# A hybrid encoder block on one core: retention rotates without the row factor, and the setup is laid out anew

## The chip, the cores and the metric

The kernel runs on one core of one Trainium2 chip. A core has a matrix engine (TensorE, PE in the profile; its weight loads are PEld), a vector engine (VectorE, DVE), an activation engine (ScalarE, ACT), a general engine (GpSimd, POOL) and an engine that here only starts transfers (SyncE, SP). Each engine takes its instructions in a fixed order. The metric is the device time of one execution, in microseconds (us).

## The reference

Sixteen learned meta tokens are put ahead of 1024 positions of width 1024 (T = 1040 rows). One layer follows: a root-mean-square norm, one combined input projection, a branch A of bidirectional retention in four heads (chunks of 128 rows), a branch B of windowed attention in eight heads, two gates, an output projection, a second norm and a residual add. Cut to what the change touches:

```python
u = _rms_norm(h, pre_w)          # row i of x*pre_w times r_i = rsqrt(mean(x_i^2) + eps)
z = u @ w_in                     # rq, rk, rv, rg, aq, ak, av, ag, gr, ga
rq = _rotary(rq, pos); rk = _rotary(rk, pos) * RET_DK ** -0.5
# retention, forward: out_i = sum_{j <= i} (q_i . k_j) * gamma^(i-j) * v_j, and backward likewise
o_r = (o_r - mean) * rsqrt(var + EPS)   # per row and head
```

The factor r_i of a row is one number, so it can be applied to the result of a projection instead of to its input.

## The kernel before

All matrix products are made from fp32 values split in a rounded high part and a remainder: `mm3` (L68) issues three matmuls, high by high (L70), low by high (L71) and high by low (L72). x stands in memory transposed, in eight blocks of 128 channels by 1040 rows. The kernel is written as one sequence of operations, and a planner at compile time gives each engine its fixed order from that sequence and its own estimate of times.

**Setup (L213 to L311).** SyncE starts all loads: the norm weights `vec`, the decay parameters `dect`, the weight of the first retention head in four parts (`w0_part`), x block by block (`xr`, six buffers), the constants `tabt` (identity, two distance tables and five index columns `idx`), and the rotation tables `cr` and `sr`. For each block k ScalarE writes the high part `xh` (L268), VectorE the low part `xl` (L269), and TensorE adds the block's share to the six outputs of head 0's keys (four pieces) and queries (two halves) (`qk0_mm`, 18 matmuls a block). Those six outputs take six of the eight accumulator banks: two of the three in the group `pj`, one of two in `p1`, both in `p2`, the one in `p3`. ScalarE also squares each block (L274), and the squares are added up in two sums, `sq[0]` on VectorE and `sq[1]` for the last three blocks, there on GpSimd (L278). 36 matmuls with a single column of ones (18 calls, L285) turn the sums into the mean square of each row, `ms`; GpSimd raises it to the power -0.5 (`rcol`, L288). The last block's `qk0_mm` stands behind that in the text.

GpSimd computes the retention decays from `dect` (`decays`, L173): two powers, a series in about twenty tiny operations on 128x8 tiles, six scaled exponents `ex`, and (`decay_columns`, L198) one power that gives the table of columns `dtab`. `decay_table` (L203) makes the 128x128 decay mask `DT` of a head from `lg`, on VectorE and ScalarE.

`rcol` is a column. For each chunk it is spread over a tile by ScalarE (`rw`) and turned by a matmul with the identity (L303) into a row over all partitions, `rbc`, which VectorE multiplies into `cr` and `sr` (L305, L306). The rotation of a projected piece (`rope_evac`, L151) then applies the row factor along with the angle: three VectorE instructions into `m1` and `m2` (two buffers each) and an add on GpSimd (L158).

**Retention (L364).** For each head: `stage1` projects a value chunk (`projT`, 24 matmuls into a `pj` bank; for chunk 0, the 16 meta rows, 16 matmuls, gathered by a ScalarE copy and a VectorE add, L138 and L139), scales it with `rcol` and splits it (`vh`, L394; `vl`, L395), turns the key chunk, forms the scores and splits them and the decayed keys. `stage2` makes the inner product, the product with the forward state and the new state. A backward sweep follows, with the per-row norm. Between the steps of the sweep `fill()` puts pieces of the next head's projection (`gen_qk`). Weights come through `load_w` in two halves, rounded on GpSimd (L75) or on ScalarE, the remainder on VectorE (L78).

After retention come attention, then four projection phases; the change does not touch them.

Of the kernel before, what the change touches and what calls it, by code (L numbers as in the profile page):

```python
# [12 lines left out]
D = 1024  # L13
SEQ = 1024
NM = 16
# [12 lines left out]
SQ2 = 5  # L28
# [11 lines left out]
def block_kernel(ctx: ExitStack, tc: tile.TileContext, xT, x, w_in, w_rb, w_ab, w_out, vecs, dec, sink,  # L40
# [36 lines left out]
    def dve_lo(o, i, hi):  # L77
        nc.vector.tensor_tensor(o, i, hi.bitcast(F32), ALU.subtract)  # L78
# [72 lines left out]
    def rope_evac(t, a, b, o, nm):  # L151
# [5 lines left out]
        nc.vector.tensor_tensor(m2[0:64, 0:n], t[64:128, 0:n], sr[64:128, a:b], ALU.mult)  # L157
        nc.gpsimd.tensor_tensor(o[:, 0:n], m1[:, 0:n], m2[:, 0:n], ALU.add)  # L158

# [5 lines left out]
    warm, ones = (ra.tile([P, 1], F32, name=n) for n in ("warm", "ones"))  # L165
    dect, neg1, neg, na, e, e2, s_, ss, acc, lg = (ra.tile([P, 8], F32, name=n) for n in (
        "dect", "neg1", "neg", "na", "e", "e2", "s_", "ss", "acc", "lg"))
    ecst, ex = (ra.tile([P, 28], F32, name=n) for n in ("ecst", "ex"))
    ms = ra.tile([P, 9], F32, name="ms")
# [3 lines left out]
    def decays():  # L173
# [3 lines left out]
        nc.vector.memset(neg1, -1.0)  # L177
# [4 lines left out]
        g.tensor_scalar(e2, e, 2.0, 1.0, op0=ALU.add, op1=ALU.mult)  # L182
        g.tensor_tensor(e2, e2, neg1, ALU.pow)
# [28 lines left out]
    pv0 = {}  # L212
    with tc.tile_pool(name="setup", bufs=1, reuse_waits="tile") as st:  # L213
        nc.sync.dma_start(vec, vecs)
        nc.sync.dma_start(dect, dec.partition_broadcast(P))
        xr = [st.tile([P, T], F32, tag="xr", bufs=6, name=f"xr{k}") for k in range(KT)]
# [15 lines left out]

        w0_part(0, 1)
        nc.sync.dma_start(xr[0][:, 0:528], xT[0, :, 0:528])
# [5 lines left out]
        nc.sync.dma_start(tabt, tab[:, MW:])  # L240
        nc.sync.dma_start(xr[3], xT[3])
        w0_part(4, 8)
        nc.sync.dma_start(xr[4], xT[4])
        nc.sync.dma_start(xr[5], xT[5])
        nc.sync.dma_start(xr[6], xT[6])
        nc.sync.dma_start(xr[7], xT[7])
# [7 lines left out]
        sq = []  # L254
# [6 lines left out]
        nc.vector.memset(ones, 1.0)  # L261
        nc.vector.memset(ms, 1.0)
        decays()
        for k in range(KT):
            t = xr[k]
            parts = [(0, 528), (528, T)] if k == 0 else [(0, T)]
            for a, b in parts:
                nc.scalar.activation(xh[k][:, a:b], t[:, a:b], AF.Copy, scale=vec[:, k:k + 1])  # L268
                nc.vector.scalar_tensor_tensor(xl[k][:, a:b], t[:, a:b], vec[:, k:k + 1], xh[k][:, a:b].bitcast(F32),  # L269
                                               op0=ALU.mult, op1=ALU.subtract)  # L270
            if k < KT - 1:
                qk0_mm(k)
            q_ = st.tile([P, T], F32, tag="sq" if k else "sq0", bufs=4 if k else 1, name=f"sq{k}")
            nc.scalar.activation(q_, t, AF.Square)  # L274
            if k in (0, SQ2):
                sq.append(q_)
            else:
                (nc.gpsimd if k > SQ2 else nc.vector).tensor_tensor(sq[-1], sq[-1], q_, ALU.add)  # L278
        decay_columns()

        pms = p1("pms")
        for c in range(9):
            a, b = cols(c)
            for i in range(2):
                nc.tensor.matmul(pms[0:b - a, c:c + 1], sq[i][:, a:b], ones, start=i == 0, stop=i == 1)  # L285
    nc.vector.tensor_scalar(ms[0:NM, 0:1], pms[0:NM, 0:1], 1.0 / D, EPS, op0=ALU.mult, op1=ALU.add)
    nc.vector.tensor_scalar(ms[:, 1:9], pms[:, 1:9], 1.0 / D, EPS, op0=ALU.mult, op1=ALU.add)
# [4 lines left out]
    wv0 = load_w(w_in, U_V, act=True)  # L292
# [1029 lines left out]
```

## Time and profile before

| | us |
|---|---|
| median of 3 runs | 1105.4 (1105.38 to 1106.14) |
| the profiled execution | 1106.03 |
| its span | 1104.3 |
| TensorE busy | 1074.6 (97%) |
| VectorE busy | 869.5 (79%) |
| ScalarE busy | 487.4 (44%) |
| GpSimd busy | 257.5 (23%) |

The span is the stretch of the profiled execution from its first to its last instruction; the time of the execution lies 1.7 us around it. A row of a timeline gives start, duration, engine, line, operation, output and inputs with their shapes, and in brackets how long the engine had stood still and which engine's work ended that. `[2.66 <-DVE w L78]` is a wait of 2.66 us that ended when VectorE had written w at line 78. The granted clock is the share of full speed that TensorE's clock had in a stretch.

### The profile page before, as it was taken

What the parts mean: (1) busy time and instruction counts of PE and PEld (TensorE: products, weight loads), DVE (VectorE), ACT (ScalarE), POOL (GpSimd) and SP (SyncE); (2) the same over time, 40 slices, a digit from 0 to 9 for tenths busy, and PEclk for the clock granted to TensorE, in tenths of its full rate; (3) what the DMA queues carried; (4) which work ended last, traced back from release to release, by engine and by line L of the source; (5) the groups of instructions that cost most, each with busy time, mean ns of one, the idle gap of its engine ahead of it and who ended that gap; (6) DMA issues with size and microseconds to landing.
All of it is one profiled execution on the core that took longest, in us unless ns stands there. A gap on an engine that the chain in (4) does not pass through costs nothing.

```text
span 1104.3 us, 17280 instructions
## 1 busy us (share of the span) xinstructions
PE 1074.6 (97%) x5994; PEld 928.2 (84%) x5994; DVE 869.5 (79%) x1840; ACT 487.4 (44%) x1131; POOL 257.5 (23%) x378
## 2 busy tenths in 40 slices
PE   6899999999999999999999999999999999999996
PEld 5799999999988988988888788888888788787885
DVE  6487887878976798988667876888889889867765
ACT  7132241422513544544557644455457546433442
POOL 7532433324232244445220000000000000010032
PEclk9799999999999999999999999999999999999999
DMA  7201111101114971021114753779883765779463
GB/s 285 77 1 39 58 58 39 46 32 63 54 48 127 350 248 58 21 96 39 65 46 158 257 200 105 229 245 338 273 290 122 229 207 191 234 199 335 119 114 77
DMA packets 75656, 159.45 MB, mean 144 GB/s; under 512 B 7985, under 2 KB 19761, under 8 KB 74801
## 3 DMA queue, kind: packets, MB, share of 16 engines
q1 hardware_dynamic: 72112, 152.06, 40.1%
q0 software_dynamic: 3456, 6.29, 3.7%
q8 instruction: 47, 0.77, 0.3%
q14 instruction: 41, 0.33, 0.1%
HBM read 105.89 MB, written 52.43 MB: 143 GB/s over the span
## 4 chain that ended last, share of the span: by engine, by line
PE 87%; DVE 4%; DMA 3%; POOL 2%; ACT 1%; issue 1%; SPq 1%; POOLq 0%; DVEq 0%; ACTq 0%
PE bz L71 7%; PE bz L72 7%; PE bz L70 7%; PE paq L71 3%; PE paq L72 3%; PE paq L70 3%; PE bo L71 2%; PE br L71 2%; PE bo L70 2%; PE bo L72 2%; PE br L72 2%; PE br L70 2%; PE pv L70 2%; PE pv L71 2%; PE pv L72 2%; PE ba L71 2%
## 5 line engine op out<-in xcount | busy, mean ns | idle before, releaser
L961 POOL DMA_DIRECT2D mx_d<-c1a x4 | 3.7, 924 | 397.6 <-DVE c1a L952 394.3
L71 PE MATMUL bz<-big,llz 128*128 128x512 f32 x208 | 82.5, 397 | 0.4 <-DVE llz L78 0.3
L72 PE MATMUL bz<-big,lhz 128*128 128x512 f32 x208 | 81.9, 394 | 0.0
L70 PE MATMUL bz<-big,lhz 128*128 128x512 f32 x208 | 81.1, 395 | 0.0
L72 PE MATMUL pv<-wl,big 128*128 128x256 f32 x256 | 73.2, 286 | 0.0
L70 PE MATMUL pv<-wh,big 128*128 128x256 f32 x256 | 73.2, 286 | 0.0
L71 PE MATMUL pv<-wh,big 128*128 128x256 f32 x256 | 72.9, 285 | 0.0
L70 PE MATMUL bz<-T,lhz 128*128 128x512 f32 x156 | 61.8, 396 | 1.7 <-ACT T L659 1.3
L71 PE MATMUL bz<-T,llz 128*128 128x512 f32 x156 | 61.5, 394 | 0.0
L72 PE MATMUL bz<-T,lhz 128*128 128x512 f32 x156 | 61.3, 394 | 0.0
L78 DVE TENSOR_TENSOR wl<-wr,wh 128x1024 fp32r<-128x1024 f32 x34 | 47.6, 1401 | 14.0 <-POOL wh L75 14.0
L1112 ACT ACTIVATE p<-p,nm 128x400 f32<-128x400 f32 (+1 forms) x64 | 38.4, 600 | 38.8 <-DVE nm L1110 35.0
L1123 POOL TENSOR_SCALAR p<-p,den 128x400 f32<-128x400 f32 (+1 forms) x60 | 36.3, 615 | 71.9 <-DVE den L1118 49.1
L71 PE MATMUL paq<-big,wl 128*128 128x512 f32 x128 | 51.3, 401 | 0.0
L70 PE MATMUL paq<-big,wh 128*128 128x512 f32 x128 | 51.0, 398 | 0.0
L72 PE MATMUL paq<-big,wh 128*128 128x512 f32 x128 | 50.9, 397 | 0.0
L70 PEld LDWEIGHTS pv<-wh,big 128*128 128x128 f32 x256 | 48.9, 191 | 0.9 <-DVE vl L395 0.6
L72 PEld LDWEIGHTS pv<-wl,big 128*128 128x128 f32 x256 | 48.8, 190 | 0.1
L71 PEld LDWEIGHTS pv<-wh,big 128*128 128x128 f32 x256 | 48.8, 191 | 0.0
L71 PEld LDWEIGHTS bz<-big,llz 128*128 128x128 f32 x208 | 39.1, 188 | 9.8 <-DVE llz L78 0.9
L70 PEld LDWEIGHTS bz<-big,lhz 128*128 128x128 f32 x208 | 39.1, 188 | 9.4 <-ACT lhz L682 0.2
L72 PEld LDWEIGHTS bz<-big,lhz 128*128 128x128 f32 x208 | 39.2, 188 | 8.9
(609 smaller groups left out, 3670.8 us busy)
## 6 DMA issues: line engine op xcount, KB each, us to landing
wr<-in_w_in_dram SPq DMA_DIRECT2D x35, 512.0 KB, 3.6
wrz<-in_w_in_dram SPq DMA_DIRECT2D x28, 512.0 KB, 5.5
tg<-tg_d SPq DMA_DIRECT2D x32, 256.0 KB, 4.4
T<-preT SPq DMA_DIRECT2D x6, 1024.0 KB, 8.6
oTr_d<-ost SPq DMA_DIRECT2D x16, 256.0 KB, 2.2
xs<-in_xT_dram SPq DMA_DIRECT2D x16, 256.0 KB, 5.0
xsT<-xs SPq DMA_DIRECT2D x16, 256.0 KB, 4.8
oTa_d<-oa SPq DMA_DIRECT2D x16, 256.0 KB, 2.2
```

The source lines that it names most:

```text
L70: nc.tensor.matmul(o, ah, bh, start=first, stop=False, **kw)
L71: nc.tensor.matmul(o, al, bh, start=False, stop=False, **kw)
L72: nc.tensor.matmul(o, ah, bl, start=False, stop=last, **kw)
L78: nc.vector.tensor_tensor(o, i, hi.bitcast(F32), ALU.subtract)
L961: nc.gpsimd.dma_start(d, to, accum_op=ALU.add)
L1112: nc.scalar.activation(p[:, 0:wid], p[:, 0:wid], AF.Exp, scale=-1.0, bias=nm_[:, e_:e_ + 1], accum_out=den[:, e_:e_ + 1])
L1123: nc.gpsimd.tensor_scalar(pt[e_][:, 0:wid], pt[e_][:, 0:wid], den[:, e_:e_ + 1], 1.0, op0=ALU.mult, op1=ALU.mult)
```

## The change

The row factor leaves the rotation of retention. Queries and keys are rotated without it; the values carry its square (`r2`, the reciprocal of the mean square, on VectorE), and the output rows carry it once: in the copy of the inner product (`scale=rcol`) and in the query decay columns (`qd`, which now hold rcol times the decay, a column for each chunk). Score (i, j) lacks r_i and r_j, value j has r_j squared, row i gets r_i back.

Around that: all squares are added up on VectorE, in one sum that is then split in high and low parts, and 18 rounded matmuls with two columns of ones replace the 36. `decay_columns` comes right behind `decays`, and the second power in `decays` becomes a reciprocal on VectorE. The first half of x's first block, `dect` and the five index columns are loaded from ScalarE's queue; the tables of `tabt` come last; x has eight buffers. Head 0's first piece is rotated ahead of the split of the sum, the other five behind it, and on VectorE everything of retention comes behind the last of these (`issue_after(ins)` keeps what is written in its block behind `ins` on the engine of `ins`). The decay mask of head h + 1 is made at chunk 4 of head h. The row `rbc` is laid out in the second head, at chunks 2, 4 and 6, now by transposes, and multiplied into `cr` and `sr` ahead of the last head, since the later users of the rotation (attention) still need it.

```diff
         g.tensor_tensor(e, ecst[:, 0:8], na, ALU.pow)
-        g.tensor_scalar(e2, e, 2.0, 1.0, op0=ALU.add, op1=ALU.mult)
-        g.tensor_tensor(e2, e2, neg1, ALU.pow)
+        nc.vector.tensor_scalar(e2, e, 2.0, None, op0=ALU.add)
+        nc.vector.reciprocal(e2, e2)
...
+    def evac_qk0(*pieces):
+        if 0 not in qk:
+            qk[0] = [], ra.tile([P, 4, 272], F32, tag="kp", bufs=2, name="kr0")
+        q, kt = qk[0]
+        for i in pieces:
+            m0, a, b, t = (outs[2:] + outs[:2])[i]
...
+            rot = rope_evac(t, a, b, o, f"qk0_{i}")
+        return rot
...
-        nc.sync.dma_start(vec, vecs)
-        nc.sync.dma_start(dect, dec.partition_broadcast(P))
-        xr = [st.tile([P, T], F32, tag="xr", bufs=6, name=f"xr{k}") for k in range(KT)]
+        xr = [st.tile([P, T], F32, tag="xr", bufs=KT, name=f"xr{k}") for k in range(KT)]
...
+        nc.scalar.dma_start(xr[0][:, 0:528], xT[0, :, 0:528])
+        nc.scalar.dma_start(dect, dec.partition_broadcast(P))
+        nc.scalar.dma_start(idx, tab[:, MW + 3 * P:])
+        nc.sync.dma_start(vec, vecs)
         w0_part(0, 1)
-        nc.sync.dma_start(xr[0][:, 0:528], xT[0, :, 0:528])
...
-        nc.sync.dma_start(tabt, tab[:, MW:])
...
         nc.sync.dma_start(sr, rope[1])
+        nc.sync.dma_start(tabt[:, 0:3 * P], tab[:, MW:MW + 3 * P])
...
         decays()
+        decay_columns()
         for k in range(KT):
...
-            if k < KT - 1:
-                qk0_mm(k)
-            q_ = st.tile([P, T], F32, tag="sq" if k else "sq0", bufs=4 if k else 1, name=f"sq{k}")
+            qk0_mm(k)
+            q_ = st.tile([P, T], F32, tag="sq", bufs=4, name=f"sq{k}")
             nc.scalar.activation(q_, t, AF.Square)
-            if k in (0, SQ2):
-                sq.append(q_)
-            else:
-                (nc.gpsimd if k > SQ2 else nc.vector).tensor_tensor(sq[-1], sq[-1], q_, ALU.add)
-        decay_columns()
-
+            if sq is not None:
+                nc.vector.tensor_tensor(q_, sq, q_, ALU.add)
+            sq = q_
+        pack_meta()
+        wv0 = load_w(w_in, U_V, act=True)
+        evac_qk0(0)
+        sqh, sql = (st.tile([P, T], R, name=n) for n in ("sqh", "sql"))
+        nc.scalar.copy(sqh, sq)
+        split = dve_lo(sql, sq, sqh)
         pms = p1("pms")
         for c in range(9):
             a, b = cols(c)
-            for i in range(2):
-                nc.tensor.matmul(pms[0:b - a, c:c + 1], sq[i][:, a:b], ones, start=i == 0, stop=i == 1)
+            for i, t in enumerate((sqh, sql)):
+                summed = nc.tensor.matmul(pms[0:b - a, 2 * c:2 * c + 2], t[:, a:b], ones, start=i == 0, stop=i == 1).ins
...
+    nc.vector.reciprocal(r2, ms)
     nc.gpsimd.tensor_tensor(rcol, ms, mhalf[:, 0:9], ALU.pow)
-    qk0_mm(KT - 1)
-    pack_meta()
...
-    vmeta = ra.tile([NM, 256], F32, name="vmeta0")
-    pv0[0] = projT(wv0, 0, "pv0_0", vmeta)
-    for g, cs in enumerate(((0, 1, 2), (3, 4, 5, 6), (7, 8))):
-        t = p1(f"rb{g}")
...
+    def row_factors(cs):
+        t = p1(f"rb{cs[0]}")
...
             nc.scalar.copy(rw[0:n], rcol[0:n, c:c + 1].to_broadcast([n, P]))
-            nc.tensor.matmul(t[:, a - base:b - base], rw[0:n], ident[0:n, 0:n], start=True, stop=True)
+            nc.tensor.transpose(t[:, a - base:b - base], rw[0:n], ident[0:n, 0:n])
         nc.scalar.copy(rbc[:, base:b], t[:, 0:b - base])
-        nc.vector.tensor_tensor(cr[:, base:b], cr[:, base:b], rbc[:, base:b], ALU.mult)
-        nc.vector.tensor_tensor(sr[:, base:b], sr[:, base:b], rbc[:, base:b], ALU.mult)
-    decay_table((0,))
+    def turn_factors():
+        for t in (cr, sr):
+            nc.vector.tensor_tensor(t, t, rbc, ALU.mult)
...
-            nc.scalar.activation(vh[0:n], pv[0:n, 0:256], AF.Copy, scale=rcol[0:n, c:c + 1])
+            state["v"] = nc.scalar.activation(vh[0:n], pv[0:n, 0:256], AF.Copy, scale=r2[0:n, c:c + 1]).ins
...
-                nc.scalar.copy(o, pa[:, 0:256])
-                nc.vector.scalar_tensor_tensor(o, pa[:, 256:512], qdf(h), o, op0=ALU.mult, op1=ALU.add)
+                nc.scalar.activation(o, pa[:, 0:256], AF.Copy, scale=rcol[:, c:c + 1])
+                nc.vector.scalar_tensor_tensor(o, pa[:, 256:512], qdf(h, c), o, op0=ALU.mult, op1=ALU.add)
...
-        if h == 0:
-            decay_table((1, 2, 3))
...
+            if c == 4 and h < NH - 1:
+                decay_table((h + 1,))
+            if h == 1 and c in (2, 4, 6):
+                with tc.issue_after(state["v"]):
+                    row_factors({2: (0, 1, 2), 4: (3, 4, 5), 6: (6, 7, 8)}[c])
             stage2(c)
...
-    evac_qk0()
+    with tc.issue_after(split):
+        evac_qk0(1, 2, 3)
+        decay_table((0,))
+        rotated = evac_qk0(4, 5)
     for h in range(NH):
...
-        retention(h, fill)
-        drain()
+        with tc.issue_after(rotated):
+            if h == 0:
+                for i, j in enumerate((8, 12)):
+                    for k in range(NH):
+                        nc.vector.tensor_scalar(qd[:, NH * i + k], rcol[:, 1:9], dtab[:, j + k:j + k + 1], None,
+                                                op0=ALU.mult)
+            if h == NH - 1:
+                turn_factors()
+            retention(h, fill)
+            drain()
```

More of the change, by code (lines that the diff above doesn't have):

```diff
@@ L27 @@
 N_GATE = 3
-SQ2 = 5
 U_QK, U_V, U_G = 0, 4, 8
@@ L164, in block_kernel @@
     mask = ra.tile([P, MW], F32, name="mask")
-    warm, ones = (ra.tile([P, 1], F32, name=n) for n in ("warm", "ones"))
-    dect, neg1, neg, na, e, e2, s_, ss, acc, lg = (ra.tile([P, 8], F32, name=n) for n in (
-        "dect", "neg1", "neg", "na", "e", "e2", "s_", "ss", "acc", "lg"))
+    warm = ra.tile([P, 1], F32, name="warm")
+    ones, onef = (ra.tile([P, 2], t, name=n) for n, t in (("ones", R), ("onef", F32)))
+    dect, neg, na, e, e2, s_, ss, acc, lg = (ra.tile([P, 8], F32, name=n) for n in (
+        "dect", "neg", "na", "e", "e2", "s_", "ss", "acc", "lg"))
     ecst, ex = (ra.tile([P, 28], F32, name=n) for n in ("ecst", "ex"))
-    ms = ra.tile([P, 9], F32, name="ms")
+    ms, r2 = (ra.tile([P, 9], F32, name=n) for n in ("ms", "r2"))
+    qd = ra.tile([P, 2 * NH, NB], F32, name="qd")
     nc.vector.memset(warm, 0.0)
@@ L259, in qk0_mm @@
                     k == 0, k == KT - 1)
-        nc.vector.memset(ones, 1.0)
+        nc.vector.memset(onef, 1.0)
+        nc.vector.tensor_copy(ones, onef)
         nc.vector.memset(ms, 1.0)
         decays()
+        decay_columns()
         for k in range(KT):
@@ L318, in kdb, with qdf, qdb @@
         return dtab[:, 4 + h:5 + h]
-    def qdf(h):
-        return dtab[:, 8 + h:9 + h]
-    def qdb(h):
-        return dtab[:, 12 + h:13 + h]
+    def qdf(h, c):
+        return qd[:, h, c - 1:c]
+    def qdb(h, c):
+        return qd[:, NH + h, c - 1:c]
     def cdf(h):
```

52 lines of the change are left out of this document (22 added, 30 removed).

## The prediction

> **What bounds the kernel now.** I read the page's busy line first, then the waits of TensorE, then a table of stretches up to 51.6 us, then the timelines of TensorE, GpSimd and VectorE inside those stretches.
>
> ```profile
> span 1104.3 us, 17280 instructions
> PE 1074.6 (97%) x5994; PEld 928.2 (84%) x5994; DVE 869.5 (79%) x1840; ACT 487.4 (44%) x1131; POOL 257.5 (23%) x378
> ```
>
> TensorE is busy for 97% of the span, so a change pays only if it takes away TensorE's idle time, slow clock or work. The waits say where the idle time is (columns: total us, times, longest):
>
> ```profile
> PE pq L70 <- ACT big L268: 7.0, 1, 7.0
> PE pms L285 <- POOL sq L278: 4.1, 1, 4.1
> PE pq L71 <- DVE w L78: 2.7, 1, 2.7
> ```
>
> All three lie in the setup, where the diff lies. The stretches (us, busy time and count of PE, PEld, DVE, ACT, POOL, granted clock, DMA) show what they cost:
>
> ```profile
> 6.90:21.10 14.20, 14.09 (x78) 12.51 (x78) 9.52 (x14) 13.59 (x14) 11.79 (x24) 1.00 1.03 406
> 21.10:23.70 2.60, 0.00 (x1) 0.01 (x1) 2.60 (x6) 1.16 (x2) 2.60 (x3) 1.00 0.53 213
> 23.70:35.50 11.80, 11.77 (x61) 10.20 (x61) 10.58 (x21) 5.10 (x8) 11.48 (x8) 0.86 0.30 98
> 35.50:39.60 4.10, 0.00 (x1) 0.01 (x1) 0.00 (x0) 0.00 (x0) 4.02 (x3) 0.77 0.28 109
> 39.60:46.60 7.00, 7.00 (x35) 6.99 (x35) 1.23 (x1) 0.00 (x0) 0.96 (x1) 0.50 0.21 75
> 46.60:51.60 5.00, 5.00 (x24) 4.13 (x24) 1.45 (x3) 0.69 (x3) 2.84 (x2) 0.52 0.00 0
> ```
>
> At 35.5 every engine but GpSimd stops while GpSimd adds squares. Then 35 one-column matmuls of the sums take 7.0 us at half clock, and the next 24 run at half clock too. Next, TensorE's timeline:
>
> ```profile
> 6.95 0.77 PE L70 MATMUL pq<-big,w 128*128 128x512 f32 x1 [6.95 <-ACT big L268]
> ...
> 11.43 0.39 PE L70 MATMUL pq<-big,w 128*128 128x512 f32 x1
> ...
> 19.93 0.63 PE L70 MATMUL pq<-big,w 128*128 128x512 f32 x2
> ...
> 23.70 0.92 PE L71 MATMUL pq<-big,w 128*128 128x512 f32 x2 [2.66 <-DVE w L78]
> ...
> 27.16 0.55 PE L70 MATMUL pq<-big,w 128*128 128x512 f32 x1
> ...
> 52.81 0.28 PE L71 MATMUL pv<-wh,big 128*128 128x256 f32 x1
> ...
> 55.41 0.28 PE L72 MATMUL pv<-wl,big 128*128 128x256 f32 x1
> ...
> 58.91 0.28 PE L70 MATMUL pv<-wh,big 128*128 128x256 f32 x1
> ```
>
> The first block of 18 matmuls takes 11.43 - 6.95 = 4.48 us (it begins cold), the next three (19.93 - 11.43) / 3 = 2.83 each. From 52.81 to 55.41 lie 22 steps: 0.118 us per 256-column matmul, so 24 of them, one value chunk, take 2.84. The fourth value chunk, c3, starts at 58.91. That is my milestone: I ask when the changed kernel starts c3, because from there on TensorE has the same work ahead of it in both.
>
> **The change part by part.**
>
> *Start.* The first half of x0 leaves on ScalarE's queue instead of fourth on SP's, and its landing no longer sets the start; the weight does:
>
> ```profile
> 5.91 0.40 POOL L75 TENSOR_SCALAR w<-wr 128x256 fp32r<-128x256 f32 x1
> ...
> 6.56 1.66 POOL L183 TENSOR_TENSOR e<-e,neg 128x8 f32<-128x8 f32 x1
> ```
>
> GpSimd has the first rounded weight at 6.31, behind the first power of the decays, which the change leaves in place; so TensorE starts at about 6.4, 0.55 earlier. The three DMAs issued on ScalarE, the two freed places in SP's queue, the eighth x buffer and the later load of the tables are costed at nothing: ScalarE's first work on data waits for x0 anyway, and x7 and the tables are read only after 20 us. If x0 lands late, the start is 6.95 again and 0.55 is lost.
>
> *The 2.7 us wait for the weight's low part.* VectorE was in order behind the decay table of all heads:
>
> ```profile
> 20.83 0.51 DVE L206 TENSOR_SCALAR dd<-tabt,lg 128x128 f32<-128x128 f32 x2 [3.73 <-POOL lg L192]
> 21.25 1.26 DVE L278 TENSOR_TENSOR sq<-sq,sq 128x1040 f32<-128x1040 f32 x1
> 22.43 1.21 DVE L78 TENSOR_TENSOR w<-wr,w 128x1024 fp32r<-128x1024 f32 x1
> ```
>
> The table now comes behind the split of the squares, so this wait goes. What could be late next is VectorE itself. It gets seven adds of squares instead of four:
>
> ```profile
> L269 DVE SCALAR_TENSOR_TENSOR big<-xr,vec,big 128x1040 fp32r<-128x1040 f32 x7 | 9.2, 1324 | 0.7 <-ACT big L268 0.7
> L278 DVE TENSOR_TENSOR sq<-sq,sq 128x1040 f32<-128x1040 f32 x4 | 5.0, 1238 | 0.0
> L126 DVE CAST xm<-big 128x64 fp32r<-128x64 f32 x4 | 0.7, 183 | 0.0
> ```
>
> From about 9 us (an estimate: TensorE was at x1's block at 11.43, and x1 leaves two places earlier in SP's queue) it has 7 x 1.32 + 7 x 1.24 + 0.7 + 1.2 (two weight splits) = 19.8 us: done at 28.9, the last split of x at 27.7. TensorE's eight blocks, unstalled, end at 6.4 + 4.48 + 7 x 2.83 = 30.7. So VectorE stays ahead by 1 to 3 us; with less than that, TensorE would wait inside the blocks, and each us of it moves the milestone only if the handover below doesn't swallow it.
>
> *Sum of squares.* Gone are the two adds on GpSimd and their wait; new is a split (one instruction each on ScalarE and VectorE, on VectorE 1.24 like an add), and 18 rounded matmuls for 36. The old ones took 7.0 / 35 = 0.20 at half clock; I take 0.1 at full clock, 1.8 us, between nothing (hidden in idle time) and 18 x 0.2 = 3.6.
>
> *Handover.* Rotation no longer waits for the row factor, but VectorE does everything of retention only after the last of six rotations. Three banks are there for value chunks: c0 at once, c1 and c2 after the first and second rotation; c3 needs c0's bank, which VectorE frees (L139) behind the sixth. So c3 starts at R = end of rotations + the eight new query-decay columns + L139:
>
> ```profile
> 46.83 0.15 DVE L287 TENSOR_SCALAR ms<-pms 128x8 f32<-128x8 f32 x1
> ...
> 52.12 0.41 DVE L139 TENSOR_TENSOR vmeta<-pv,vmeta 16x256 f32<-16x256 f32 x1 [0.96 <-ACT vmeta L138]
> ...
> 54.33 0.43 DVE L155 TENSOR_TENSOR m_qk<-pk,cr 128x272 f32<-128x272 f32 x1
> ...
> 69.21 0.67 DVE L155 TENSOR_TENSOR m_qk<-pq,cr 128x512 f32<-128x512 f32 x1
> ```
>
> A rotation of a key piece is three such instructions, 1.3 us, of a query half 2.05. By VectorE alone: 28.9, four packing casts 0.7 and two value-weight splits 2.4 (32.0), first rotation 33.3, split 34.5, three rotations 3.9, sums and table 1.4 (an estimate: seven small instructions at about 0.2), two query rotations 4.1 (43.9), columns 1.2 and L139 0.4: R = 45.5.
>
> But each rotation ends in an add on GpSimd with two buffers, so the third rotation needs the first add, and GpSimd is busy with the decays:
>
> ```profile
> 10.39 1.18 POOL L185 TENSOR_TENSOR ss<-s__114 128x8 f32<-128x8 f32 x1
> ...
> 15.94 1.12 POOL L189 TENSOR_SCALAR acc<-acc 128x8 f32<-128x8 f32 x1
> ...
> 17.44 0.20 POOL L189 TENSOR_SCALAR acc<-acc 128x8 f32<-128x8 f32 x1
> ...
> 20.90 7.00 POOL L194 TENSOR_SCALAR ex<-lg,tabt 128x4 f32<-128x4 f32 x5
> 27.87 1.26 POOL L196 TENSOR_SCALAR ex<-lg 128x8 f32<-128x8 f32 x1
> 29.21 4.85 POOL L199 TENSOR_TENSOR dtab<-ecst,ex 128x28 f32<-128x28 f32 x1
> ...
> 55.75 0.77 POOL L158 TENSOR_TENSOR kr<-m_qk,m_qk 128x272 f32<-128x272 f32 x1 [5.85 <-DVE m_qk L157]
> ```
>
> A tiny operation takes 1.1 to 1.4 us while VectorE works and 0.20 while it stands still (it stood waiting from 17.1 to 20.8). In the changed kernel VectorE doesn't stand still. One power of 1.66 is gone, so ss comes at 8.7; it and 18 more operations at 1.12 end at 30.0. Of the six exponents three go at 1.4 (34.2); VectorE then soon waits for GpSimd, the rest run fast (35.2); the power 4.85 and two scales end at 40.5. First add 41.3; third rotation 42.6, fourth 43.9; the query rotations wait for the adds of these two, 46.0 and 48.1; plus 1.6: R = 49.5, taking rcol's power as fitting between.
>
> On this point the Trainium skill (GPSIMD Engine Reference, Specifications) says that GpSimd shares its SBUF interfaces with VectorE, with contention where VectorE reads two SBUF inputs. By that rule moving the squares to VectorE slows the decays put first on GpSimd, and the time is that of R = 49.5; if it didn't hold here, R = 45.5. The 1.12 against 0.20 above agrees with it.
>
> TensorE meanwhile has c0 (16 matmuls, 1.9), c1, c2 (2.84 each) and the sums (1.8): done at 30.7 + 9.4 = 40.1. It then idles for 9.4 us and restarts cold. The price of that: 12 matmuls after the 2.7 us wait took 27.16 - 23.70 = 3.46 against 2/3 x 2.83 = 1.89, so 1.6.
>
> *Row factors.* Nine transposes in the second head cost 9 x 0.118 = 1.1 on TensorE; their copies run on ScalarE (44% busy). Between nothing and 2.5 (if each comes cold).
>
> *VectorE later.* The factors' turn into the rotation tables at the last head is two instructions of 1.24; the tables of the other heads move inside the heads. I cost them at nothing because VectorE has gaps (79%); if the cover is gone it is 2.5.
>
> Sum: c3 earlier by 58.9 - 49.5 = 9.4, less 1.6 cold, less 1.1 transposes: 6.7 us. The profiled execution took 1106.03 us around its span of 1104.3, and the median of the runs, 1105.4, is 0.6 below it: 1106.0 - 6.7 - 0.6 = 1098.7.
>
> **The rivals.**
> 1. GpSimd doesn't hold the rotations (the adds stand ahead of the exponents in its queue, or these run faster): R = 45.5, gain 10.7, 1094.7. For it: VectorE's order alone allows it. Against it: decays come first in the program. Were TensorE never to wait (c3 at 40.1), the gain would be 17.7, 1087.7.
> 2. Given back at the head boundaries: the 2.5 us of the factors' turn, in front of the last head, fall on the chain. The three waits above are the only ones over 1.3 us of TensorE, which speaks for slack there; gain 4.2, 1101.2.
> 3. Slower: GpSimd's decays get slower still. One exponent took up to 2.66 us by the tile's view:
>
> ```profile
> L194 POOL TENSOR_SCALAR ex<-lg,tabt x5: 360/1319/2655, 20.9 to 25.2; 128x4 f32<-128x4 f32 x5
> ```
>
> Six at that price end at 46, the power at 51.2, R = 60.2, and c3 is 1.3 later than now: with 1.6 and 1.1 that is 4.0 slower, 1109.4. It decides when the decays end after 47.2 (R = 56.2); slower than the measurement can miss, after 49.4.
>
> **How the numbers follow.** Likeliest, as summed, 0.42 (own range 1096.5 to 1100.5); rival 1 0.27, TensorE never waiting 0.04; rival 2 0.13; rival 3 0.14, of which 0.03 within 0.2%. 0.2%, 2.2 us, is about what a measurement of this kernel tells from no change. Of rival 2, 0.02 is within that too. Faster 0.84, same 0.05, slower 0.11. The range runs from 1089.0 (most of rival 1) to 1104.5 (rival 2 and a little of rival 3), leaving 0.05 below and 0.14 above.
>
> **What would show it.** Right: TensorE starts near 6.4 and has no wait on w; eight blocks end near 31; the sums take under 2.5 us; then one wait of 4 to 10 us, released by VectorE's L139 or a value split, with VectorE itself waiting on GpSimd's adds; from c3 on waits as before. Wrong: TensorE waiting inside the eight blocks (VectorE too late with the splits), no wait at the handover, or new waits of over 1 us at the second and fourth head.

## The result, and the profile after

The changed kernel takes 1098.7 us (median of four runs, 1097.02 to 1099.49) against 1105.8 for the kernel before beside it (1105.38 to 1107.58): a ratio of 0.9931, with an interval of 0.9914 to 0.9948. The profiled execution took 1098.83 us around its span. Its busy line:

```profile
span 1097.0 us, 17210 instructions
PE 1069.3 (97%) x5967; PEld 923.3 (84%) x5967; DVE 873.3 (80%) x1851; ACT 490.2 (45%) x1132; POOL 258.5 (24%) x374
```

Of the 7.3 us that the span lost, 5.3 are TensorE's busy time (1074.6 to 1069.3), 2.0 its idle time. The largest waits of TensorE in the setup and at the handover to retention (total us, times, longest):

```profile
PE pq L69 <- POOL w L74: 4.6, 1, 4.6
PE tr L408 <- DVE m_qk L156: 2.8, 1, 2.8
PE pkv L71 <- DVE vl L405: 1.4, 1, 1.4
...
PE pv L69 <- DVE vmeta L138: 1.2, 2, 1.0
```

The wait for squares on GpSimd (4.1 us before) and the wait for the weight's low part (2.7) are gone (0.2 us of the latter is left); the 4.6 us are the start. The same stretches as a table (us, busy time and count of PE, PEld, DVE, ACT, POOL, granted clock, DMA):

```profile
4.50:30.90 26.40, 26.05 (x146) 23.02 (x147) 23.71 (x33) 19.32 (x20) 23.09 (x24) 1.00 0.74 289
...
35.70:37.60 1.90, 1.90 (x20) 1.88 (x19) 0.08 (x1) 0.00 (x0) 1.90 (x1) 1.00 0.00 0
...
38.40:41.50 3.10, 0.29 (x4) 0.12 (x3) 1.40 (x4) 0.00 (x0) 3.10 (x4) 1.00 0.00 0
41.50:45.00 3.50, 3.50 (x18) 3.50 (x18) 3.35 (x8) 1.03 (x3) 1.74 (x3) 0.53 0.00 0
45.00:48.40 3.40, 1.08 (x5) 0.46 (x4) 3.28 (x8) 0.37 (x1) 2.74 (x2) 0.98 0.02 5
48.40:55.00 6.60, 6.27 (x35) 5.81 (x35) 6.60 (x19) 2.09 (x6) 4.82 (x4) 0.74 0.47 156
```

The eight blocks run with 0.35 us of idle time, the sums take 1.8 us at full clock (35.78 to 37.60). Then TensorE stands still for 2.8 us, works 3.5 us at half clock, stands still for 2.3 us more in three pieces (0.69 us for the row sums, 0.70 for a rotated query, 0.99 for the add of the first value chunk), and runs slow again behind c3. The clock column reads 1.00 for the first block too, although its 256-column matmuls come 0.21 us apart there (8.53 to 8.95) and not 0.118, so it leaves the slow start out. TensorE's timeline:

```profile
4.56 0.76 PE L69 MATMUL pq<-big,w 128*128 128x512 f32 x1 [4.56 <-POOL w L74]
...
37.49 0.25 PE L305 MATMUL pms<-ones,sql 128*128 128x2 f32 x1
...
41.49 0.27 PE L408 MATMUL tr<-ident,kr 128*16 128x128 f32 x1 [2.81 <-DVE m_qk L156]
...
48.45 0.53 PE L69 MATMUL pv<-wh,big 128*128 128x256 f32 x1 [0.99 <-DVE vmeta L138]
```

c3 starts at 48.45, 10.45 us earlier than before (58.91). What held it there is read on GpSimd and on VectorE:

```profile
13.42 1.12 POOL L190 TENSOR_SCALAR acc<-acc 128x8 f32<-128x8 f32 x1
...
28.14 1.05 POOL L193 TENSOR_TENSOR lg<-lg,acc 128x8 f32<-128x8 f32 x1
...
32.79 4.82 POOL L200 TENSOR_TENSOR dtab<-ecst,ex 128x28 f32<-128x28 f32 x1
...
38.24 1.05 POOL L74 TENSOR_SCALAR wh<-wr 128x1024 fp32r<-128x1024 f32 x1
39.25 0.75 POOL L157 TENSOR_TENSOR kr<-m_qk,m_qk 128x272 f32<-128x272 f32 x1
```

```profile
40.04 0.42 DVE L154 TENSOR_TENSOR m_qk<-pk,cr 128x256 f32<-128x256 f32 x1 [4.26 <-POOL kr L157]
...
47.99 0.41 DVE L138 TENSOR_TENSOR vmeta<-pv,vmeta 16x256 f32<-16x256 f32 x1
...
51.60 0.19 DVE L309 RECIPROCAL r<-ms 128x9 f32<-128x9 f32 x1
52.67 1.59 DVE L651 TENSOR_SCALAR qd<-rcol,dtab 128x8 f32<-128x8 f32 x8
```

Decays at 1.1 us an operation, the power of the columns, the rounding of half of the next head's weight (1.05 us, not in the forecast), then the first add (done at 40.0), for which VectorE's third rotation waited 4.26 us; the add of the first value chunk (L138) right behind the last rotation.

The lead of 10.45 us is not the gain of 7.1 (1105.8 to 1098.7). Followed by the first matmul of each piece of later work, it is 4.4 us at head 1's keys, 10.4 at head 2's, 11.1 at head 3's (220.01 to 208.93), and only 6.0 at attention's keys (287.44 to 281.47); from there it stays at 6 to 7. A first matmul also moves when the planner changes the order, so one such lead alone says little (the two kernels lose next to nothing between the first two of these, and the lead still goes from 4.4 to 10.4). The drop from 11.1 to 6.0 is different: the loss there can be seen. It lies at the start of the last head. The stretch from 250 to 290 us holds it in both kernels; first before, then after, with TensorE's waits there:

```profile
250.00:290.00 40.00, 39.52 (x319) 37.66 (x318) 34.69 (x92) 13.86 (x40) 15.50 (x24) 1.00 0.21 67
```

```profile
250.00:290.00 40.00, 37.66 (x285) 36.20 (x284) 32.83 (x98) 15.85 (x49) 12.84 (x23) 0.91 0.18 63
```

```profile
PE to L491 <- DVE rs L521: 1.0, 1, 1.0
PE pb L69 <- DVE rs L521: 0.7, 1, 0.7
PE tr L408 <- ACT ost L496: 0.6, 1, 0.6
```

Before, 0.5 us of this stretch is idle. After, 2.3 us are idle and 37.66 us of work run at a mean clock of 0.91, 3.4 us lost: 5.7 against 0.5.

### The profile page after: what moved, and what is told of

Read it like the earlier page. It is cut to its first block, busy times and chain, and to the rows that moved or that the text cites. A ratio compares the mean times of both kernels' runs of the same rounds, so it can differ in the third digit from the quotient of the medians.

```text
span 1097.0 us, 17210 instructions
## 1 busy us (share of the span) xinstructions
PE 1069.3 (97%) x5967; PEld 923.3 (84%) x5967; DVE 873.3 (80%) x1851; ACT 490.2 (45%) x1132; POOL 258.5 (24%) x374
## 4 chain that ended last, share of the span: by engine, by line
PE 83%; DVE 7%; POOL 3%; DMA 3%; ACT 2%; issue 2%; SPq 1%; POOLq 0%; DVEq 0%; ACTq 0%
PE bz L70 7%; PE bz L71 7%; PE bz L69 7%; PE br L70 2%; PE bo L70 2%; PE bo L69 2%; PE br L69 2%; PE bo L71 2%; PE br L71 2%; PE paq L70 2%; PE paq L71 2%; PE paq L69 2%; PE ba L70 2%; PE ba L71 2%; PE ba L69 2%; PE pv L69 2%
## 5 line engine op out<-in xcount | busy, mean ns | idle before, releaser
L69 PE MATMUL pv<-wh,big 128*128 128x256 f32 x256 | 75.1, 293 | 1.3 <-DVE vmeta L138 1.2
L70 PE MATMUL pv<-wh,big 128*128 128x256 f32 x256 | 74.2, 290 | 0.0
L69 PEld LDWEIGHTS pv<-wh,big 128*128 128x128 f32 x256 | 50.4, 197 | 2.4 <-DVE vmeta L138 1.6
L70 PEld LDWEIGHTS pv<-wh,big 128*128 128x128 f32 x256 | 50.4, 197 | 0.0
```

The source lines that it names most:

```text
L69: nc.tensor.matmul(o, ah, bh, start=first, stop=False, **kw)
L70: nc.tensor.matmul(o, al, bh, start=False, stop=False, **kw)
```

## The experiments

All times of a run are set against the kernel before on the same chip; the intervals are of the ratio. One table for all of them, explained by the sections below. "Lost" is TensorE's idle time plus its busy time times one minus the granted clock, added up over windows of 1 us in the profiled execution, at four places: the setup (0 to 60 us), the start of the last head (250 to 290), the end of retention (340 to 365), and the first projection phase (590 to 700). "Cover" below is work of another piece that TensorE can do while a step waits for another engine.

| run | ratio [interval] | span | c3 | lost 0-60 | 250-290 | 340-365 | 590-700 |
|---|---|---|---|---|---|---|---|
| before | 1 | 1104.3 | 58.9 | 21.3 | 0.5 | 2.1 | 2.1 |
| changed | 0.9931 [0.9914, 0.9948] | 1097.0 | 48.5 | 14.7 | 5.7 | 1.5 | 2.1 |
| a0 changed, again | 0.9941 [0.9928, 0.9954] | 1097.7 | 48.8 | 15.5 | 5.3 | 1.8 | 2.1 |
| e1 turn late | 0.9945 [0.9932, 0.9957] | 1098.1 | 48.2 | 16.7 | 5.6 | 1.5 | 2.1 |
| e8 turn forced late | 0.9988 [0.9976, 1.0000] | 1104.2 | 48.4 | 16.7 | 3.7 | 6.4 | 5.5 |
| e13 the same, cover held | 0.9929 [0.9912, 0.9946] | 1095.6 | 48.2 | 15.6 | 2.1 | 4.0 | 2.1 |
| e2 spare buffers | 0.9990 [0.9979, 1.0001] | 1104.8 | 49.8 | 16.5 | 5.3 | 5.0 | 4.8 |
| e9 and splits behind | 1.0004 [0.9994, 1.0015] | 1104.2 | 46.7 | 13.5 | 5.2 | 5.0 | 6.5 |
| e15 the same, cover held | 0.9938 [0.9922, 0.9954] | 1098.9 | 46.0 | 12.1 | 5.8 | 2.5 | 2.5 |
| e10 both | 0.9919 [0.9906, 0.9933] | 1095.4 | 46.2 | 12.3 | 2.1 | 5.0 | 2.8 |
| e12 both, cover held | 0.9901 [0.9883, 0.9919] | 1093.6 | 46.0 | 12.8 | 2.1 | 3.8 | 2.1 |
| e5 reciprocal early | 0.9968 [0.9959, 0.9978] | 1099.0 | 48.4 | 15.2 | 4.0 | 5.1 | 2.1 |
| e3 no adds of squares | one run, 1098.13 us | 1096.3 | 44.7 | 12.5 | 4.0 | 5.0 | 2.3 |
| e4 sum not split | 0.9955 [0.9940, 0.9970] | 1099.5 | 51.2 | 17.0 | 4.3 | 4.0 | 2.1 |

Span less the four losses is 1071.8 to 1074.0 us in all runs of the changed program but one (e15, 1076.0), so these four places explain the spans within about 1 us of each other. Each row is one profiled execution: the setup's order is the same in the changed kernel, a0, e1, e8 and e13, and it lost 14.7 to 16.7 us there, so differences of 1 to 2 us at one place can come from the execution and not from the edit.

### The changed kernel again

> The changed kernel once more, beside the next three on the same chip, so that they can be set against it directly. All theories: 1098.7 us, within 0.7.

1099.58 us (1098.31 to 1100.05), 0.9941: 0.2 us above the expected range. The intervals of the two ratios overlap, so a difference of 0.1% between two runs is not read as an effect below.

### The turn of the row factors, put late (e1, e8, e13)

```diff
-            if h == NH - 1:
-                turn_factors()
             retention(h, fill)
...
+            if c == 4 and h == NH - 1:
+                turn_factors()
```

> The two VectorE instructions that turn the row factors into the rotation tables stand at the fifth chunk of the last head and no longer ahead of its first. Theory A (they delay VectorE's first work for the last head, and TensorE's several short idle times around 262 to 268 us, 2.3 us, and the half clock after them, 268 to 274 us, some 2.9 us, follow from that): 4 to 5 us faster than the changed kernel, 1094.2 (1093.5 to 1095.0), and idle and half clock there gone. Rival B (the loss at the last head comes from the order of the rest, the turn only lies beside it): 1098.7, within 0.7, and the same idle time at the last head with the turn gone from it.

1099.78 us: no change from the second measurement. But the planner had put the two instructions back to where they were, as VectorE's timeline of this run shows (245.53 and 248.47 in the changed kernel), so it tells nothing of theory A:

```profile
246.70 1.43 DVE L332 TENSOR_TENSOR cr<-cr,rbc 128x1040 f32<-128x1040 f32 x1
...
249.64 1.22 DVE L332 TENSOR_TENSOR sr<-sr,rbc 128x1040 f32<-128x1040 f32 x1
```

So the place was forced, behind the scaled values of the sixth chunk:

```diff
+            if c == 4 and h == NH - 1:
+                with tc.issue_after(state["vl"]):
+                    turn_factors()
```

> The same edit as in the run of the turn put late, but now held on VectorE behind the scaled values of the sixth chunk of the last head, since there the planner had put the two instructions back ahead of that head. With it the order on TensorE at the last head is again that of the kernel before: ten more matmuls of value chunks between the last products of the backward sweep. Theory A (the turn, 2.65 us of VectorE, late for the sweep, makes the planner use up TensorE's cover early, and the 2.3 us idle and 3.4 us of slow clock at the last head are its price): that stretch costs under 1 us, and the time is 4 to 5 us less than the changed kernel's, 1094.6 (1093.5 to 1096.0). Rival B (the loss there has nothing to do with the turn, or is replaced by another at the turn's new place): 1098.9, within 0.8.

1105.17 us, slower than the changed kernel by 0.5%, which neither theory gives. At the last head it did what theory A says, in part: the loss fell from 5.3 to 3.7 (2.1 of idle time, 1.6 of slow clock). TensorE's order there shows how (name, chunk and number of matmuls; `pb` are the products of head 2's backward sweep, `pv` head 3's value chunks, which are the cover):

```
before   pb_3x3 to_5x1 pv_6x16 to_4x1 pb_2x3 to_3x1 tr_0x1 pb_1x3
changed  pb_3x3 to_5x1 pv_6x6 to_4x1 pb_2x3 pb_1x3 to_3x1 tr_0x1
forced   pb_3x3 pv_5x5 pv_6x2 to_5x1 pv_6x10 to_4x1 pv_6x4 pb_2x3 pv_6x8 to_3x1 tr_0x1 pb_1x3
```

In the changed kernel the turn sits in the middle of the sweep's start: its first two products stand at 242.75 and 250.94, 8.2 us apart (256.91 and 260.31 before, 3.4 apart), and 62 matmuls of cover go in between. At the sweep's end, where each step waits for the norm of a chunk, 6 are left for 16. Then, in the forced run, two later places lost 8.0 us more:

```profile
PE to L494 <- DVE op L526: 2.7, 2, 2.5
PE po L69 <- ACT pbh L1180: 2.0, 1, 2.0
```

```profile
340.00:365.00 25.00, 21.80 (x157) 20.95 (x156) 16.38 (x42) 13.40 (x31) 3.08 (x8) 0.86 0.68 230
590.00:700.00 110.00, 106.20 (x477) 85.63 (x476) 83.44 (x151) 60.33 (x120) 0.30 (x1) 0.98 0.52 177
```

The order shows these two as well. At the end of retention the last head's last product had no cover behind it (`pav` is attention's value projection), and the first projection (`bz`) began when attention's blocks `po_4` to `po_7` were still to do; in the changed kernel, `po_6` and `po_7`:

```
changed  pb_1x3 pavx5 to_3x1 pavx10 to_2x1 pavx7 to_1x1 ps_0x2
forced   to_3x1 pavx3 pb_1x3 to_2x1 to_1x1 ps_0x2
```

Nothing in the edit touches either place; the planner works out one order for the whole program and came to another. The next run holds the cover there, twelve matmuls of the third value chunk behind the last `pb`:

```diff
         for k in range(KT):
-            mm3(t[0:b - a, 0:256], ...
+            with tc.issue_after(last_pb[0]) if k >= hold else ExitStack():
+                mm3(t[0:b - a, 0:256], ...
```

> The run with the turn held late (1105.2), and now twelve matmuls of the attention's third value chunk are held on TensorE behind the last product of the last head's backward sweep; with them TensorE's order from there to the first projection phase is the changed kernel's again. Theory A (the turn's late place did help at the last head, and the 8 us that run lost came from two later places, 3.4 us idle with 2.7 us of slow clock around 346 to 356 us and the first projection begun before the attention's third last block): at the last head the lead of 1 us over the changed kernel is kept to the end, 1098.4 (1097.6 to 1099.2). Rival B (the loss has another cause, which the twelve matmuls don't touch): 1103 or more.

1098.89 us beside 1107.3 of before: 0.9929 [0.9912, 0.9946], in theory A's range. At the first projection the order is the changed kernel's again, and the 590 to 700 us loss is back at 2.1. At the end of retention it is not quite: the last `pb` has the twelve matmuls behind it, where the changed kernel has 22, and a wait of 1.3 us is left. At the last head the slow clock is gone, but not by this edit: TensorE's order and its waits there are those of the run before (two of 0.9 us and two of 0.2), which were followed by 1.6 us of slow clock in that execution and by none in this one.

```profile
250.00:290.00 40.00, 37.88 (x307) 36.31 (x306) 36.32 (x99) 17.70 (x56) 13.69 (x22) 1.00 0.15 54
340.00:365.00 25.00, 22.74 (x175) 22.02 (x174) 14.51 (x35) 14.51 (x33) 2.82 (x6) 0.93 0.77 265
```

```profile
PE to L497 <- DVE op L529: 1.3, 1, 1.3
```

From head 3's keys to attention's keys this run takes 69.6 us, the changed kernel's second run 72.2, and the loss from 250 to 290 us is 3.2 us less (1.6 in the run before). So the turn in its old place, with the order that came of it, costs 1.6 to 3.2 us. But 2.2 us are lost again at the end of retention (4.0 for 1.8), and the times of the two can't be told apart.

### No wait for GpSimd's first add (e2, e9, e15)

```diff
-        m1 = ra.tile([P, 512], F32, tag="m1", bufs=2, name=f"m1_{nm}")
-        m2 = ra.tile([P, 512], F32, tag="m2", bufs=2, name=f"m2_{nm}")
+        if spare:
+            m1, m2 = o, ra.tile([P, 512], F32, tag="q", bufs=6, name=f"m2_{nm}")
...
+            rot = rope_evac(t, a, b, o, f"qk0_{i}", i in (2, 3))
```

> The rotations of the third and fourth key piece of head 0 write their products into the output and into a spare buffer, so that they need not wait for GpSimd's first add (40.0 us, behind the decays). Theory A (this wait of 4.3 us on VectorE sets the end of the rotations and with it the start of the fourth value chunk c3): the two rotations run at 35.5 to 38.2, the query rotations from 40.0 to 44.2, c3 starts at about 44.6 for 48.45, and the time is 3.9 us less than the changed kernel's, 1094.8 (1094.0 to 1095.8). Rival B (something else holds the query rotations or c3, GpSimd's adds above all, or the lead is spent at a head's boundary): c3 at 46.5 or later, or c3 early and the time still 1097.5 to 1099.

1104.97 us, and c3 at 49.81, later than without the edit: neither theory's time, and rival B's late c3. The rotations did end at 44.2, as theory A says; then the planner put other work ahead of the row sums and L138, and TensorE waited 6.88 us behind it. VectorE's timeline (this kernel's L159 is the rotation):

```profile
43.51 0.69 DVE L159 TENSOR_TENSOR m_qk<-pq,sr 64x512 f32<-64x512 f32 x1
...
44.44 3.83 DVE L77 TENSOR_TENSOR wl<-wr,wh 128x1024 fp32r<-128x1024 f32 x2
...
49.06 0.40 DVE L138 TENSOR_TENSOR vmeta<-pv,vmeta 16x256 f32<-16x256 f32 x1
```

So the two splits at 44.44 (head 1's weights) were held behind L138:

```diff
-        w = load_w(w_in, U_QK + h)
+        with tc.issue_after(meta_done[0]):
+            w = load_w(w_in, U_QK + h)
```

> The spare buffers of the run before, and the low parts of the next head's key and query weights are held on VectorE behind the add that closes the first value chunk (they took 3.8 us between rotations and that add in the run with spare buffers alone). Theory A (there the rotations did end 3.7 us early, and only these splits took the wait's place): rotations end at 44.2, c3 starts at 45.0 to 46.0 (48.45 in the changed kernel), and the time is 2.0 to 3.5 us less than the changed kernel's, 1096.0 (1095.0 to 1097.5). Rival B (a third work takes the place, or the lead is lost at a head's boundary): c3 after 47, or c3 early and the time 1098 or more.

c3 at 46.66 and a lead over the changed kernel of 1.7 to 2.9 us up to attention, as theory A says; and 1106.75 us, since the two later places lost 7.6 us more than in the changed kernel's second run: rival B, at boundaries that lie 300 and over 540 us behind the edit. With the cover held:

> The run with spare buffers and the later splits (1106.8), with the same twelve matmuls held. Theory A (a start of c3 that is 2.2 us earlier is worth about that, as long as the order after retention is the changed kernel's): c3 at 46.7, and 2.2 to 2.9 us less than the changed kernel's 1099.6, 1097.0 (1096.0 to 1098.0). Rival B (the boundaries swallow it whatever the order): 1098.9 or more.

0.9938: no gain that can be told from the changed kernel (1100.58 us beside 1107.3 of before), rival B's time. The order at the first projection is the changed kernel's, the lead at attention's first value chunk is 2.6 us, and at the output phase 0.2. The windows show 1.1 us of that loss (340 to 365 and 590 to 700); where the rest went stays open. One more microsecond lies behind TensorE's last matmul, 9.6 us from the end in this execution and 8.6 in the changed kernel's two.

### Both (e10, e12)

> Both edits of the two runs beside it. Theory A (two separate losses): the gains add up, 6 to 8 us less than the changed kernel, 1092.0 (1090.5 to 1094.0). Rival B (what is won at the handover is lost again at a later boundary): no better than the better of the two alone, within 0.8.

1098.13 us, 0.9919 [0.9906, 0.9933]: 7 us better than either run alone, and 6 short of theory A, so neither theory's number. The planner came to the good order for attention's end by itself here (590 to 700: 2.8), but not for the end of retention (5.0). With the cover held:

> The run with both edits (1098.1), with the same twelve matmuls held; everything of the two runs beside it together. Theory A: at the attention's first value chunk that run was 5.9 us ahead of the changed kernel, then 3.4 us idle and 1.6 us of slow clock around 341 to 348 took 4 of it; with the cover there the lead stays, 1094.0 (1093.0 to 1095.5). Rival B (the lead is lost again at the next place): 1097 or more.

1096.05 us, 0.9901 [0.9883, 0.9919], c3 at 45.95: the fastest of all, 0.4% below the changed kernel's second measurement, with intervals that don't overlap (that of its first one just touches). It lies between theory A's range and rival B's, 2 us short of theory A's 1094.0 on the face of it; against its own before (1107.3 where the others had 1106.0) about 1. The two gains add up as far as attention's first value chunk, where the lead over the changed kernel's second run is 6.2 us, against 3.9 with the turn alone (e13) and 2.6 with the spare buffers alone (e15). Behind that 2.0 us are lost again at the end of retention (3.8 for 1.8), and the span is 4.1 us shorter.

### The reciprocal early (e5)

```diff
-        rotated = evac_qk0(4, 5)
+        with tc.issue_after(inverse):
+            rotated = evac_qk0(4, 5)
```

> The two query rotations of head 0 come behind the reciprocal of the row sums, which ran only at 51.6 us in the changed kernel although its matmuls ended at 37.6; the values' scaling needs it. Theory A (this late reciprocal is what TensorE's wait of 1.4 us for the first scaled values at 56.2 comes from): reciprocal before 46, that wait under 0.5, 1097.5 (1097.0 to 1098.2). Rival B (the scaled values were late for VectorE's queue, not for the reciprocal): reciprocal early, the wait still over 1 us, 1098.7 within 0.7.

1102.16 us, 0.3% slower. The reciprocal runs at 43.6 (52.0 in the changed kernel's second run) and TensorE no longer waits for the scaled values; but in that second run it waited only 0.27 us for them with the reciprocal just as late, so the 1.44 us of the first profile isn't the reciprocal's alone, and which theory holds stays open. c3 is at 48.4, nothing is gained at the handover, and the end of retention has lost its cover (5.1 for 1.8); neither theory gives that time.

### VectorE without the adds of squares (e3)

```diff
-            if sq is not None:
-                nc.vector.tensor_tensor(q_, sq, q_, ALU.add)
```

> VectorE's seven adds of squares are left out, so that only the last block's squares enter the row factor; else as the changed kernel. Theory A (GpSimd's tiny operations take 1.1 us instead of 0.2 because VectorE reads two operands beside them): many of the 128x8 operations from 9 to 29 us fall to 0.2, their sum ends at 24 or earlier instead of 29.2, and the decay columns by 33 or earlier instead of 38.2; rotations end 4 us earlier or more. Rival B (it is GpSimd's own time, whatever VectorE does): they stay at 1.1 and the columns end at 38.

The column power starts at 24.72 instead of 32.79 and the columns end at 30.1 instead of 38.2: theory A. The last rotation ends at 41.6, 6.4 us earlier; then the planner puts the eight query-decay columns (2.60 us) ahead of L138, and c3 comes at 44.69, 3.8 us earlier. VectorE also has 8.7 us less to do here (seven adds at 1.24), so only the times of GpSimd's operations, not all of c3's, speak for the cause. GpSimd's and VectorE's timelines side by side show that the price isn't a slower operation but a wait for the end of VectorE's instruction:

```profile
13.55 0.20 POOL L189 TENSOR_TENSOR acc<-acc,ss 128x8 f32<-128x8 f32 x1
13.84 1.28 POOL L190 TENSOR_SCALAR acc<-acc 128x8 f32<-128x8 f32 x1
15.20 0.20 POOL L189 TENSOR_TENSOR acc<-acc,ss 128x8 f32<-128x8 f32 x1
15.49 0.20 POOL L190 TENSOR_SCALAR acc<-acc 128x8 f32<-128x8 f32 x1
15.77 1.17 POOL L189 TENSOR_TENSOR acc<-acc,ss 128x8 f32<-128x8 f32 x1
```

```profile
13.76 1.30 DVE L285 SCALAR_TENSOR_TENSOR big<-xr,vec,big 128x1040 fp32r<-128x1040 f32 x1 [0.64 <-ACT big L284]
14.98 0.31 DVE L125 CAST xm<-big 128x64 fp32r<-128x64 f32 x2
15.65 1.23 DVE L77 TENSOR_TENSOR w<-wr,w 128x1024 fp32r<-128x1024 f32 x1 [0.37 <-ACT w L241]
```

The operation begun at 13.84 ends at 15.12, VectorE's at 15.06; the one begun at 15.77 ends at 16.94, VectorE's at 16.88. Between them they take 0.20. The time of the single run, 1098.13, is about the changed kernel's: of the 3.8 us the end of retention took 3.2 (5.0 for 1.8).

### The sum not split (e4)

```diff
-        nc.scalar.copy(sqh, sq)
-        split = dve_lo(sql, sq, sqh)
...
-            for i, t in enumerate((sqh, sql)):
-                summed = nc.tensor.matmul(pms[0:b - a, 2 * c:2 * c + 2], t[:, a:b], ones, start=i == 0, stop=i == 1).ins
+            nc.tensor.matmul(pms[0:b - a, 2 * c:2 * c + 2], sq[:, a:b], onef, start=True, stop=True)
```

> The changed kernel with the sum of squares not split: nine plain fp32 calls for the eighteen rounded matmuls, and no split on ScalarE and VectorE (1.32 us); the same twelve matmuls held. Theory A (the split costs VectorE nothing that counts, since VectorE waits 4.3 us for GpSimd right behind it, and plain fp32 matmuls at full clock cost 0.1 us each like the rounded ones): sums 1.5 to 2.0 us, c3 at 48.4 within 0.7, time 1099.6 within 1. Rival B (without the rounding the sums are long again): 3.5 us or more on TensorE. Rival C (the split was on the path): c3 at 47.2 or earlier and 1.2 us less time.

1101.84 us, 0.9955. Theory A is right on the sums (18 matmuls from 31.35 to 33.29) and wrong on c3 and on the time, and neither rival holds. TensorE's timeline, and behind it VectorE's:

```profile
31.35 2.08 PE L304 MATMUL pms<-onef,sq 128*16 128x2 f32 x18
...
51.23 0.55 PE L69 MATMUL pv<-wh,big 128*128 128x256 f32 x1 [3.47 <-DVE vmeta L140]
```

```profile
48.03 2.61 DVE L650 TENSOR_SCALAR qd<-rcol,dtab 128x8 f32<-128x8 f32 x8
50.67 0.41 DVE L140 TENSOR_TENSOR vmeta<-pv,vmeta 16x256 f32<-16x256 f32 x1
```

Eighteen plain fp32 matmuls (two for each one written) took 1.9 us, eighteen rounded ones 1.8, so the sums' 7.0 us became 1.8 by one sum instead of two and by the clock, not by the rounding. The row factor being ready earlier, the planner put the eight query-decay columns ahead of the chunk's add, where they cost 2.6 us; in the changed kernel they stand at 52.67, behind it.

## Why the prediction was right, and where it was not

The number is right. Of its steps, the handover up to c3 is right in cause and within 1.05 us in size; the start and the form of the wait were not as said, and the step behind c3 failed.

*Start.* The weight's rounding did not stay behind the first power: TensorE began at 4.56 and not at 6.4. The decay parameters, now on ScalarE's queue, came later (VectorE waited for them until 5.23, before until 3.80), so GpSimd rounded the weight first. It gained nothing, since the first block then took 6.33 us (until 10.89) where the forecast had 4.48; the blocks end at 30.9, as said (30.7).

*Waits inside the blocks, and the sums.* Right: 0.35 us of idle time, and 1.8 us for the sums.

*Handover.* The mechanism is the one forecast: decays slowed by VectorE hold the first add, the add holds the third rotation. Sizes: `lg` at 29.2 (30.0), columns at 38.2 (40.5, since the last exponents ran at 0.24), first add 40.0 (41.3, without the rounding of 1.05 us that stood ahead of it), last rotation 47.95 (48.1), and the eight columns came behind L138 and not ahead of it. So c3 is at 48.45 for 49.5, 1.05 us better. Rival 1 is out: the wait of 4.26 us names the add. Without the adds of squares on VectorE the columns came 8 us earlier, which shows what slowed the decays; with spare buffers in place of that wait the rotations ended 3.75 us earlier (44.2 for 47.95), which shows that the add held them.

*One wait of 9.4 us.* Wrong in form. The planner put the first key's transpose, whose bank the third rotation frees, into the middle of chunk c2, so TensorE stood still from 38.4 with 17 of its matmuls undone. The price of restarting cold came twice: 3.50 x 0.47 = 1.6 us before c3, inside the lead, and 6.27 x 0.26 = 1.6 behind it, which is the 1.6 of the sum. "From c3 on waits as before" failed too: TensorE waited 1.44 us at 56.2 for the first scaled values, a term that the sum doesn't have (0.27 in the second run).

*"From there on TensorE has the same work ahead of it in both", and the factors' turn costed at nothing.* This failed. The work is the same, its cover is not. At the boundaries of the first heads (80 to 250 us) the kernel before lost 3.2 us and the changed one 0.7, a gain of 2.5 not in the sum; at the last head 5.7 for 0.5, a loss of 5.2 not in it either. Rival 2 named the place and the cause, but as 2.5 us in series.

```profile
80.00:250.00 170.00, 168.45 (x1252) 159.22 (x1251) 137.65 (x342) 52.70 (x156) 55.78 (x84) 0.99 0.13 44
```

```profile
80.00:250.00 170.00, 169.25 (x1271) 159.72 (x1271) 134.04 (x323) 51.20 (x151) 57.63 (x84) 1.00 0.15 48
```

What the traces show: the turn stands between the sweep's first steps, TensorE meanwhile uses its cover, and at the sweep's end come idle pieces of 0.6 to 1.0 us and the slow clock behind them. With the turn moved away that order is gone, and the loss is 1.6 to 3.2 us smaller (2.1 to 3.7 in the four runs with the turn moved, 4.0 to 5.8 in the others of the changed program). So the turn is shown as the cause of that part of the 5.2 only; 2.1 us of idle time stay in all four runs with the turn moved, mostly waits for the decayed keys, and their cause is open.

*Sum.* 10.45 - 1.6 (cold behind c3) - 1.4 (the wait at 56.2) - 1.1 (transposes, the forecast's figure, not measured apart) + 2.5 - 5.2 = 3.6; the lead measured at attention's keys is 6.0, and 7.3 at the end. A part of these 2.4 us is work that the changed kernel had done ahead of c3 (four transposes, from 41.49 to 46.97); the rest, and the 1.3 us won behind attention's keys, stay open. The terms that the forecast's 6.7 lacks (1.05, -1.4, 2.5 and -5.2) come to -3.1 and were made up by gains that no term of it names, so the exact agreement is luck by about 3 us; the direction and the size of the handover are not.

*What no run shows.* The setup lost 21.3 us before and 14.7 after. That the waits for GpSimd's squares and for the weight's low part went, and that the sums run at full clock, is read from the two traces; no run takes the parts of the change back one by one, so what the row factor's leaving, the single sum and the new order of loads gave each stays open.

## What to carry to other kernels

Where a planner orders the whole program, a lead won in one stage arrives at the end only if each later boundary keeps its cover: follow the lead from milestone to milestone, and read the order at the boundaries before an experiment is read by its time. Two edits here that won 1 to 3 us at their own place came out 5.6 and 7.2 us worse than the changed kernel; with twelve matmuls held in place, 90 and 300 us further on, they came back to its time, and only together below it. Work moved "into the gaps" of an engine is to be placed by the serial chain that runs there, not by the engine's share of busy time.

## What the runs showed of the hardware

- A GpSimd operation on 128x8 that met a VectorE instruction on two tensors in SBUF ended 0.05 to 0.07 us after that instruction (it takes 0.20 us otherwise); so behind VectorE's unbroken 1.2 us instructions it came to 1.1 us each. One exponent (128x4, 29.30 to 31.59 in the changed kernel) got through only behind the second of two such instructions (the last add of squares, then a weight split that ended at 31.53). Beside a rotation, whose instructions read one operand from an accumulator (31.45 to 32.8), three exponents took 0.73 together. The Trainium skill (GPSIMD Engine Reference, Specifications) tells of contention with VectorE instructions of two SBUF inputs; both halves agree with it, and the size is that of a wait for the whole instruction.
- An idle time of 2.8 us (38.7 to 41.5) was followed by half clock for 3.5 us, one of 2.5 us with two of 0.4 and 0.3 behind it (346 to 351 in e8) by half clock for over 6, and three pieces of 0.6 to 1.0 us within 4 us (263 to 267 in the changed kernel) by half clock for over 6. Pieces of 0.2 and 0.9 us within 3 us were followed by half clock for some 3 us in e8 (264.7 to 267.5, then 268 to 271), and the same pieces at the same place of the order by none in e13, e10 and e12, so the length of the pieces alone doesn't decide it. The Trainium skill (TensorE: Matmul & The Clock Gate, Part 1) gives an idle window of about 3.4 us; here shorter ones were enough.
